# First pair of a seven-product feed-forward: evictions between weight sums, early tiles, another product order, and down weights prepared one pair later

## The chip, the cores and the metric

One core of a Trainium2 chip runs the kernel. The core has a matrix engine (PE; its weight loads are listed as PEld), a vector engine (DVE), a scalar engine (ACT), a slower general engine (POOL) and queues that start transfers between device memory and on-chip memory (here nearly all from SP). Each engine works through its own list of instructions in order and waits where an operand isn't ready. The metric is the device time of one launch in microseconds, the median of several runs.

## The reference, cut to what matters

```python
h = rms_norm(x, norm1_w) * (1.0 + scale1) + shift1
x = x + gate1 * hybrid_mixer(h, w_in, ..., w_out)      # ends in  concat[A, B] @ w_out
h = rms_norm(x, norm2_w) * (1.0 + scale2) + shift2
x = x + gate2 * swiglu(h, w_gate, w_up, w_down)
return rms_norm(x, norm_f_w)

def swiglu(h, w_gate, w_up, w_down):
    return (jax.nn.silu(h @ w_gate) * (h @ w_up)) @ w_down
```

One sequence of 1024 tokens, model width 1024, feed-forward width 2816, all in float32. The change lies where the mixer's output projection ends and the gate and up projections begin, and it touches the preparation of `w_down`.

## The kernel before

The residual stream x is held transposed after the mixer, as eight tiles of 128 features by 1024 tokens; `x2h(m, hf)` is feature tile m in token half hf (512 tokens). The page of the profile prints them as `x`.

**Products.** The gate and up projections run in 11 pairs of column tiles (256 of 2816 columns; p is the pair, q is 0 for gate and 1 for up). Each pair is a 2 by 2 block product done with seven block products instead of eight: four input blocks of the weights (A11, A12, A21, A22) and their sums S1 = A21 + A22, S2 = S1 - A11, S3 = A11 - A21, S4 = A12 - S2, against four blocks of the activations (B11, B21 from token half 0; B22 from token half 1) and their differences T1, T2, T3, T4. A float32 operand is split into a rounded high half (ACT: a CAST or an ACTIVATE) and a rest (DVE: a subtraction, called its low half below); three matmuls, high by high, high by low, low by high, make one product of a 128-row block. A block product is 24 matmuls: two q, four row blocks k, three parts.

**Accumulators.** `X`, `Y`, `Z` and `V` name pairs of PSUM banks (one for each q). X takes A11·B11, is copied out (`p1`), goes on summing S2·T2, is copied again (`u2`), then S3·T3 (`z5`) and A22·T4. V takes S1·T1 in the first pair only; Y takes A12·B21, Z takes S4·B22. `keep` copies a bank out on ACT, `close` adds a bank on DVE, `silu` and `act` make silu(gate) times up; the results go to device memory (`am_scr`), also as sums.

**The first pair** (lines 2000 to 2128 of before) is written out by hand, since its activations are made while it runs. The last two of eight column tiles of the output projection (`w_out_t`, 24 matmuls each; `o` in the profile) run on PE while DVE forms the weight sums. `evict` adds a finished column tile to x in token half 1 and lets ACT square it; `add_sq` adds the square to `sq`. After the eighth, four small matmuls sum the squares of the token half over features (`row_sums`, tile `ss`), `row_root` takes the inverse root, and a matmul spreads it (`row_bc`, tile `RS`). Then `scale` normalises a tile, and `t_make` makes B22 and the T blocks with their halves. Low halves are queued in `low_q` and issued by `lows(n)`, which leaves n pending. `run0` issues a block product in a given order of (q, k); `hooks` puts work after the given matmul.

**Later pairs** run seven steps s through `run` and `block(p, s)`; the code of step s + 1's operands is issued behind step s. In each pair from 1 on, `prep_load`, `prep_gate` and `prep_sums` prepare two row blocks of `w_down` (4 loads, 4 multiplications by the gate, 4 subtractions, 7 stores to `bm_scr`), for pair p - 1. The eleventh preparation lies in the down projection.

**The down projection** runs 21 steps n (three chunks of 4, 4 and 3 pairs, seven products each), each of four slots of 12 or 9 matmuls (`dn`); operands come back from `am_scr` and `bm_scr`, three steps ahead, and are split one step later. A product's add into `xo` on DVE comes one slot after it. `flush` issues the pending stores.

All the order around the change is that of the code; nothing reorders it.

## Time and profile before

| | |
|---|---|
| median of 3 runs | 1168.71 us (1168.21 to 1169.12) |
| the profiled execution, its own time | 1169.62 us |
| its span, first to last instruction | 1167.8 us |
| PE busy in the span | 1147.9 us (98%) |
| DVE busy | 955.1 us (82%) |
| ACT busy | 565.6 us (48%) |
| mean granted TensorE clock | 0.994 |

Rows of the timeline give the start of a run of like instructions, how long it lasts, the engine, the operation, the tile written and the tiles read, their number, and in brackets how long the engine was idle before and what released it. Windows give the busy time of each engine in a stretch, the granted clock (PEclk, 1.00 is full), and the share of the transfer engines in use.

### The profile page before, as it was taken

What the parts mean: (1) busy time and instruction counts of PE and PEld (TensorE: products, weight loads), DVE (VectorE), ACT (ScalarE), POOL (GpSimd) and SP (SyncE); (2) the same over time, 40 slices, a digit from 0 to 9 for tenths busy, and PEclk for the clock granted to TensorE, in tenths of its full rate; (3) what the DMA queues carried; (4) which work ended last, traced back from release to release, by engine and by line L of the source; (5) the groups of instructions that cost most, each with busy time, mean ns of one, the idle gap of its engine ahead of it and who ended that gap; (6) DMA issues with size and microseconds to landing.
All of it is one profiled execution on the core that took longest, in us unless ns stands there. A gap on an engine that the chain in (4) does not pass through costs nothing.

```text
span 1167.8 us, 16828 instructions
## 1 busy us (share of the span) xinstructions
PE 1147.9 (98%) x5606; PEld 961.3 (82%) x5606; DVE 955.1 (82%) x1882; ACT 565.6 (48%) x1238; POOL 55.9 (5%) x85
## 2 busy tenths in 40 slices
PE   8999999999999999989899999999999999999997
PEld 7878888988888988866788888888888888888886
DVE  6799887898998875777998788887888797788676
ACT  6689732658734642244444433443344465443343
POOL 2010101001100001000000000000000000000002
PEclk9999999999999999999999999999999999999999
DMA  9823456443455570620455666556655599969413
GB/s 370 329 74 126 152 175 202 142 147 121 128 162 164 172 253 28 118 99 1 154 188 171 195 221 214 177 160 207 230 190 158 181 316 385 330 206 340 144 36 144
DMA packets 162056, 213.38 MB, mean 183 GB/s; under 512 B 54449, under 2 KB 79025, under 8 KB 161969
## 3 DMA queue, kind: packets, MB, share of 16 engines
q1 hardware_dynamic: 159568, 211.72, 55.1%
q8 instruction: 44, 0.72, 0.3%
q10 hardware_dynamic: 2400, 0.59, 0.2%
q14 instruction: 44, 0.35, 0.1%
HBM read 154.58 MB, written 57.67 MB: 182 GB/s over the span
## 4 chain that ended last, share of the span: by engine, by line
PE 92%; DVE 4%; ACT 2%; issue 1%; DMA 0%; POOL 0%; SPq 0%; ACTq 0%
PE acc L87 33%; PE acc L448 25%; PE dn L87 17%; PE o L87 4%; PE o L448 4%; PE A L448 1%; PE K L448 1%; DVE x L88 1%; DVE xo L88 1%; PE w L448 1%; PE u L448 1%; PE qk L448 1%; PE kk L448 1%; PE O L448 1%; DMA x<-in_x_dram 0%
## 5 line engine op out<-in xcount | busy, mean ns | idle before, releaser
L448 PE MATMUL acc<-h,u 128*128 128x512 f32 x1200 | 296.9, 397 | 0.3 <-ACT pr L448 0.3
L448 PEld LDWEIGHTS acc<-h,u 128*128 128x128 f32 x1200 | 220.2, 188 | 43.4 <-ACT pr L448 0.8
L87 PE MATMUL acc<-h,hl 128*128 128x512 f32 x552 | 132.3, 395 | 0.2 <-DVE h L88 0.2
L87 PE MATMUL acc<-T,hl 128*128 128x512 f32 x528 | 127.5, 394 | 3.2 <-ACT cc L88 2.2
L87 PEld LDWEIGHTS acc<-h,hl 128*128 128x128 f32 x552 | 104.2, 190 | 23.0 <-issue 1.0
L87 PEld LDWEIGHTS acc<-T,hl 128*128 128x128 f32 x528 | 98.9, 190 | 24.3 <-ACT cc L88 2.6
L87 PE MATMUL acc<-h,u 128*128 128x512 f32 (+1 forms) x504 | 97.5, 344 | 0.0
L87 PEld LDWEIGHTS acc<-h,u 128*128 128x128 f32 x504 | 82.9, 189 | 12.6
L88 DVE TENSOR_TENSOR xo<-xo,dn 128x512 f32<-128x512 f32 x84 | 57.2, 686 | 41.8 <-PE dn L87 32.9
L87 PE MATMUL dn<-h,h 128*128 128x512 f32 x396 | 90.7, 389 | 0.0
L87 PEld LDWEIGHTS dn<-h,h 128*128 128x128 f32 x396 | 74.3, 188 | 15.4
L448 ACT CAST u<-raw 128x512 fp32r<-128x512 f32 x69 | 42.8, 620 | 63.6 <-PE acc L448 57.4
L88 DVE TENSOR_TENSOR cc<-cc,acc 128x512 f32<-128x512 f32 x68 | 42.6, 648 | 30.1 <-PE acc L87 30.1
L87 PE MATMUL acc<-T,u 128*128 128x512 f32 x264 | 63.3, 392 | 2.2 <-ACT T L88 1.3
L448 DVE TENSOR_TENSOR u<-raw,u 128x512 fp32r<-128x512 f32 x82 | 56.2, 687 | 11.1 <-ACT u L448 11.1
L87 PEld LDWEIGHTS acc<-T,u 128*128 128x128 f32 x264 | 49.3, 188 | 14.5 <-ACT T L88 2.7
L448 DVE SCALAR_TENSOR_TENSOR cv<-pr,cols_a,cv 128x512 f32<-128x512 f32 x72 | 53.3, 747 | 0.5 <-ACT cv L448 0.4
L88 ACT ACTIVATE cc<-cc 128x512 f32<-128x512 f32 x33 | 20.8, 633 | 67.6 <-DVE cc L88 67.6
L88 ACT CAST hl<-S 128x512 fp32r<-128x512 f32 x42 | 24.1, 622 | 60.3 <-DVE S L88 54.9
L88 ACT CAST u<-R 128x512 fp32r<-128x512 f32 (+1 forms) x62 | 35.3, 587 | 35.2 <-DVE R L88 35.0
L88 ACT CAST h<-rw 128x512 fp32r<-128x512 f32 x57 | 32.7, 617 | 40.5 <-PE dn L87 34.6
L88 DVE TENSOR_TENSOR hl<-S,hl 128x512 fp32r<-128x512 f32 x42 | 27.3, 689 | 26.5 <-ACT hl L88 26.5
(355 smaller groups left out, 2115.4 us busy)
## 6 DMA issues: line engine op xcount, KB each, us to landing
raw<-in_w_in_dram SPq DMA_DIRECT2D x82, 256.0 KB, 3.1
am_scr<-cc SPq DMA_DIRECT2D x77, 256.0 KB, 5.2
raw<-in_w_mod_dram SPq DMA_DIRECT2D x64, 256.0 KB, 3.2
rw<-am_scr SPq DMA_DIRECT2D x55, 256.0 KB, 5.3
rw<-bm_scr SPq DMA_DIRECT2D x53, 256.0 KB, 5.3
bm_scr<-raw SPq DMA_DIRECT2D x51, 256.0 KB, 5.5
R<-in_w_gate_dram SPq DMA_DIRECT2D x22, 512.0 KB, 4.2
R<-in_w_up_dram SPq DMA_DIRECT2D x22, 512.0 KB, 5.4
```

The lines of the kernel that those rows point to most:

```text
L87: return call(*a, **k)
L88: ins = call(*a, **k)
L448: ins = call(*a, **k)
```

## The change

In the first pair the last two evictions move up between the weight sums: the seventh right after S2, the eighth after S4's halves. The differences S3 are formed later, after the squares. Empty tiles (`room`) are named first in the new pool, which settles which addresses the later tiles get; S1's, S3's and S2's halves get tiles of their own (`cast_in`). The root and its spreading no longer sit between the matmuls of A11·B11 but behind it. After S4·B22 the product S1·T1 runs before S2·T2, so all T1 blocks are made before the T2 blocks. The order of (q, k) inside a product is 00, 01, 10, 11, 02, 03, 12, 13. X is copied to `z5` during T4, into two `raw` tiles. The closing of the first pair's Y and Z (`rest0`) moves from before pair 1 into step 1 of pair 1. The preparation of `w_down` is shifted by one pair: none in pair 1, and two instead of one in the down projection (loads at n = 7 and 9, multiplications and sums at 8 and 10, stores at 9 and 11).

```diff
     elif s == 1:  (in block)
                 if p < 2:
                     keep(p, "p1", "X")
+                if p == 1:
+                    rest0()
                 w.cast("S1", 0)
...
-            prep_gate(p - 1)
+            if p > 1:
+                prep_gate(p - 2)
...
-            prep_sums(p - 1)
+            if p > 1:
+                prep_sums(p - 2)
...
+    for tag, shape, bufs in [("S", [P, 2, 4, P], 2)] * 2 + [(f"T2_{k}", [P, 2, HT], 1) for k in range(4)] + [("L", [P, 2, HT], 1)] + \
+            [(f"{n}_{k}", [P, 2, HT], 1) for n in ("T3", "T4") for k in range(4)]:
+        mp.tile(shape, F32R if tag[0] == "T" else F32, name=nm("room"), tag=tag, bufs=bufs)
...
-    for n in ("S1", "S2", "S4", "S3"):
-        W[0].sum_n(n)
-        if n in ("S2", "S4"):
-            cast0(n, 0)
-            cast0(n, 1)
-    lows()
-    evict(M_ORD[6], ps_o[6])
...
-    ACT.activation(warm, ones[:, 0:1], AF.Sqrt)
-    add_sq()
-    evict(M_ORD[7], ps_o[7])
-    add_sq()
-    run0("A11", "B11", b0["X"], True, hooks={12: lambda: row_sums(1, 7), 20: lambda: (row_root(1), row_bc(1, 6))})
+    W[0].sum_n("S1")
+    W[0].sum_n("S2")
+    cast_in("S2", 0, "T4_0")
+    cast_in("S2", 1, "T4_1")
+    evict(M_ORD[6], ps_o[6])
+    W[0].sum_n("S4")
+    cast_in("S4", 0, "T4_2")
+    cast_in("S4", 1, "T4_3")
+    ACT.activation(warm, ones[:, 0:1], AF.Sqrt)
+    lows(2)
+    add_sq()
+    lows(1)
+    evict(M_ORD[7], ps_o[7])
+    lows()
+    add_sq()
...
+    turns = [(0, 0), (0, 1), (1, 0), (1, 1), (0, 2), (0, 3), (1, 2), (1, 3)]
+    cast_in("S1", 1, "T3_3")
+    lows()
+    W[0].sum_n("S3")
+    W[0].cast("S1", 0)
+    run0("A11", "B11", b0["X"], True, hooks={12: lambda: row_sums(1, 7)})
+    row_root(1)
+    row_bc(1, 6)
+    cast_in("S3", 0, "S", 2)
...
+    for n, make in enumerate((t1, t2, t3, t4)):
+        for k in range(4):
+            make(k)
+            lows(1)
+            if k == 0 and n == 1:
+                run0("S1", "T1", b0["V"], True, turns)
+            elif k == 0 and n == 2:
+                run0("S2", "T2", b0["X"], False, turns)
+            elif k == 1 and n == 2:
+                keep(0, "u2", "X")
+            elif k == 0 and n == 3:
+                run0("S3", "T3", b0["X"], False, turns)
+            elif k == 1 and n == 3:
+                c[0]["z5"] = [raw_t(), raw_t()]
+                for q in (0, 1):
+                    ACT.copy(c[0]["z5"][q], b0["X"][q])
...
+    def rest0():
+        close(0, "p1", "Y")
+        silu(0, "p1")
+        close(0, "u2", "Z")
+        silu(0, "u2")
+        act(0, "p1")
+        dma(am_scr[0, A_IX["A11"]], c[0]["p1"][0])
+        act(0, "u2")
...
-                prep_load(p - 1)
+                if p > 1:
+                    prep_load(p - 2)
...
+        if n in (7, 9) and i == 0:
+            prep_load(NP - 2 + (n == 9), ring)
...
+        if n in (8, 10) and i == 0:
+            prep_gate(NP - 2 + (n == 10))
+        if n in (8, 10) and i == 2:
+            prep_sums(NP - 2 + (n == 10), ring)
+        if n in (9, 11) and i == 0:
             flush()
```

On DVE, before, this stood between the weight sums S2 and the root of the norm. `R` are loaded weights (the rows that write R form S4 and S3 in place), `u` low halves of S2 and S4, `sq` the sum of squares, `x<-o` an eviction:

```order
L88 TENSOR_TENSOR R_5341<-R_5341,S_5348 128x4x128
L88 TENSOR_TENSOR R_5342<-R_5342,S_5348 128x4x128
L88 TENSOR_TENSOR R_5337<-R_5337 128x4x128
L88 TENSOR_TENSOR R_5338<-R_5338 128x4x128
L88 TENSOR_TENSOR u_5351<-S_5348,u_5351 128x512
L88 TENSOR_TENSOR u_5353<-S_5348,u_5353 128x512
L88 TENSOR_TENSOR u_5357<-R_5341,u_5357 128x512
L88 TENSOR_TENSOR u_5359<-R_5342,u_5359 128x512
L88 TENSOR_TENSOR sq_5047<-sq_5047,raw_5329 128x512
L88 SCALAR_TENSOR_TENSOR x_2_4570<-o_5277,mod_c,x_2_4570 128x512
L88 TENSOR_TENSOR sq_5047<-sq_5047,raw_5369 128x512
L88 SCALAR_TENSOR_TENSOR x_3_4571<-o_5302,mod_c,x_3_4571 128x512
```

And now, at the same place:

```order
L88 TENSOR_TENSOR sq_5047<-sq_5047,raw_5329 128x512
L88 SCALAR_TENSOR_TENSOR x_2_4570<-o_5277,mod_c,x_2_4570 128x512
L88 TENSOR_TENSOR R_5341<-R_5341,S_5360 128x4x128
L88 TENSOR_TENSOR R_5342<-R_5342,S_5360 128x4x128
L88 TENSOR_TENSOR u_5366<-S_5360,u_5366 128x512
L88 TENSOR_TENSOR u_5368<-S_5360,u_5368 128x512
L88 TENSOR_TENSOR sq_5047<-sq_5047,raw_5372 128x512
L88 TENSOR_TENSOR u_5376<-R_5341,u_5376 128x512
L88 SCALAR_TENSOR_TENSOR x_3_4571<-o_5302,mod_c,x_3_4571 128x512
L88 TENSOR_TENSOR u_5378<-R_5342,u_5378 128x512
L88 TENSOR_TENSOR sq_5047<-sq_5047,raw_5386 128x512
L88 TENSOR_TENSOR u_5406<-S_5361,u_5406 128x512
```

The seventh eviction moved ahead of six instructions, the eighth ahead of one of them and of the two that form S3, which now come later.

On ACT, before, in the same stretch (`u<-S` and `u<-R` are the high halves of S2 and S4, `raw<-x` squares an evicted tile; the brackets list the engines whose signals an instruction waits for):

```order
L88 CAST u_5351<-S_5348 128x512 [waits DVE_49,PE_49,Activation_49]
L88 CAST u_5353<-S_5348 128x512 [waits DVE_49,PE_49]
L88 CAST u_5357<-R_5341 128x512 [waits DMAHW0_49,DVE_49,PE_49]
L88 CAST u_5359<-R_5342 128x512 [waits DMAHW1_49,DVE_49]
L88 ACTIVATE raw_5369<-x_2_4570 128x512 [waits DMAHW4_49,DMAHW3_49,DMAHW5_49,DMAHW2_49,DVE_49]
L88 ACT_TABLE_LOAD
```

And now:

```order
L88 CAST u_5366<-S_5360 128x512 [waits DVE_49,Activation_49]
L88 CAST u_5368<-S_5360 128x512 [waits DVE_49,Activation_49]
L88 ACTIVATE raw_5372<-x_2_4570 128x512 [waits DMAHW4_49,DMAHW3_49,DMAHW5_49,DMAHW2_49,DVE_49]
L88 CAST u_5376<-R_5341 128x512 [waits DMAHW0_49,DVE_49]
L88 CAST u_5378<-R_5342 128x512 [waits DMAHW1_49,DVE_49,Pool_49]
L88 ACT_TABLE_LOAD
```

The square moved ahead of two casts, and the first three casts lost their wait for PE.

On DVE, before, this stood where token half 1 is normalised further (`x<-x,mod_c,RS` is `scale`; `x<-x` is the difference T1, `raw<-x,x` the difference T2, `T<-raw` the low half of T2):

```order
L88 TENSOR_TENSOR x_0_4568<-x_0_4568 128x512
L88 TENSOR_TENSOR raw_5499<-x_4_4572,x_0_4568 128x512
L88 SCALAR_TENSOR_TENSOR x_1_4569<-x_1_4569,mod_c,RS_5419 128x512
L88 SCALAR_TENSOR_TENSOR T_978_5501<-raw_5499,mod_c,T_978_5501 128x512
L88 TENSOR_TENSOR x_1_4569<-x_1_4569 128x512
L88 TENSOR_TENSOR raw_5510<-x_5_4573,x_1_4569 128x512
```

And now (`h<-x` is the low half of T1):

```order
L88 TENSOR_TENSOR x_0_4568<-x_0_4568 128x512
L88 SCALAR_TENSOR_TENSOR x_1_4569<-x_1_4569,mod_c,RS_5447 128x512
L88 TENSOR_TENSOR x_1_4569<-x_1_4569 128x512
L88 SCALAR_TENSOR_TENSOR x_2_4570<-x_2_4570,mod_c,RS_5447 128x512
L88 TENSOR_TENSOR h_1_997_5525<-x_0_4568,h_1_997_5525 128x512
L88 TENSOR_TENSOR x_2_4570<-x_2_4570 128x512
```

The T2 differences and their low halves left this place; the T1 low halves, which stood behind them, moved up to it.

More of the change, by code (lines that the diff above doesn't have):

```diff
@@ L2013, in run0, with w_low, cast_in @@
                     hooks[n_mm]()
-    def cast0(n, q):
-        if n in ("S2", "S4"):
-            u = mp.tile([P, 2, 4, P], F32R, name=nm("u"), tag="T4_" + str(q + (2 if n == "S4" else 0)), bufs=1)
-            n_slot[0] += 1
-            ACT.copy(u[:, 0], W[0].m[n][q])
-            W[0].u.setdefault(n, [None, None])[q] = u
-        else:
-            W[0].cast(n, q)
-        low_q.append(lambda: W[0].low(n, q))
-    for n in ("S1", "S2", "S4", "S3"):
-        W[0].sum_n(n)
-        if n in ("S2", "S4"):
-            cast0(n, 0)
-            cast0(n, 1)
+    def w_low(n, q):
+        low_q.append(lambda: W[0].low(n, q))
+    def cast_in(n, q, tag, bufs=1):
+        u = mp.tile([P, 2, 4, P], F32R, name=nm("u"), tag=tag, bufs=bufs)
+        n_slot[0] += 1
+        ACT.copy(u[:, 0], W[0].m[n][q])
+        W[0].u.setdefault(n, [None, None])[q] = u
+        w_low(n, q)
+    W[0].new("S2")
+    W[0].new("S1")
+    W[0].sum_n("S1")
[11 more added lines that the diff above has]
+    evict(M_ORD[7], ps_o[7])
     lows()
-    evict(M_ORD[6], ps_o[6])
+    add_sq()
     for d in spill:
@@ L2034 @@
     spill.clear()
-    ACT.activation(warm, ones[:, 0:1], AF.Sqrt)
-    add_sq()
-    evict(M_ORD[7], ps_o[7])
-    add_sq()
-    dma(*spill.pop())
-    b0 = {n: [bank_tile(2 * j + q, "acc") for q in (0, 1)] for j, n in enumerate("XY")}
-    run0("A11", "B11", b0["X"], True, hooks={12: lambda: row_sums(1, 7), 20: lambda: (row_root(1), row_bc(1, 6))})
+    b0 = {n: [bank_tile(2 * j + q, "acc") for q in (0, 1)] for j, n in enumerate("XYZ")}
+    b0["V"] = [bank_tile(6 + q, "acc") for q in (0, 1)]
+    bk[0] = [{n: b0[n][q] for n in "XYZ"} for q in (0, 1)]
+    turns = [(0, 0), (0, 1), (1, 0), (1, 1), (0, 2), (0, 3), (1, 2), (1, 3)]
[7 more added lines that the diff above has]
+    cast_in("S3", 0, "S", 2)
+    W[0].low("S1", 0)
+    lows()
     run0("A12", "B21", b0["Y"], True)
-    for q in (0, 1):
-        cast0("S1", q)
     lows()
@@ L2048 @@
         t_make("B22", k, x2h(4 + k, 1), b2c[:, 4 + k:5 + k])
-        if k < 3:
-            scale(5 + k, 1)
-        lows(1)
-    turns = [(q, k) for k in range(4) for q in (0, 1)]
-    b0["Z"] = [bank_tile(4 + q, "acc") for q in (0, 1)]
-    bk[0] = [{n: b0[n][q] for n in "XYZ"} for q in (0, 1)]
-    for k in range(4):
-        scale(k, 1)
+        scale(5 + k if k < 3 else 0, 1)
         lows()
-        if k == 0:
-            run0("S4", "B22", b0["Z"], True, turns)
+    run0("S4", "B22", b0["Z"], True, turns)
@@ L2060, with t1, t2 @@
+    keep(0, "p1", "X")
+    ACT.activation(warm, ones[:, 0:1], AF.Silu)
+    def t1(k):
         g0, g1 = x2h(k, 0), x2h(k, 1)
         DVE.tensor_tensor(g0, g1, g0, ALU.subtract)
+        if k < 3:
+            scale(k + 1, 1)
+        t_make("T1", k, g0)
+    def t2(k):
         tm[k] = raw_t()
-        DVE.tensor_tensor(tm[k], x2h(4 + k, 1), g0, ALU.subtract)
+        DVE.tensor_tensor(tm[k], x2h(4 + k, 1), x2h(k, 0), ALU.subtract)
         t_make("T2", k, tm[k], b2c[:, 4 + k:5 + k])
-        if k == 0:
-            keep(0, "p1", "X")
@@ L2067, with t3 @@
-    ACT.activation(warm, ones[:, 0:1], AF.Silu)
-    for k in range(4):
-        t_make("T1", k, x2h(k, 0))
-        lows(1)
-        if k == 0:
-            run0("S2", "T2", b0["X"], False, turns)
-    b0["V"] = [bank_tile(6 + q, "acc") for q in (0, 1)]
-    keep(0, "u2", "X")
-    for k in range(4):
+    def t3(k):
         g1 = x2h(k, 1)
         DVE.scalar_tensor_tensor(g1, x2h(4 + k, 1), db2[:, k:k + 1], g1, ALU.add, ALU.subtract)
-        if k == 0:
-            lows()
-            run0("S1", "T1", b0["V"], True, turns)
@@ L2081, with t4 @@
         t_make("T3", k, g1)
-        if k in (0, 1):
-            cast0("S3", k)
-        lows(1)
-    for k in range(4):
+    def t4(k):
         DVE.tensor_tensor(tm[k], x2h(4 + k, 0), tm[k], ALU.subtract)
-        if k == 0:
-            lows()
-            run0("S3", "T3", b0["X"], False)
         t_make("T4", k, tm[k])
-        if k in (0, 1):
-            cast0("A22", k)
-        lows(1)
+    for n, make in enumerate((t1, t2, t3, t4)):
[14 more added lines that the diff above has]
+                    ACT.copy(c[0]["z5"][q], b0["X"][q])
+            if n == 1 and k == 2:
+                cast_in("S3", 1, "S", 2)
+            if n == 3 and k == 0:
+                for q in (0, 1):
+                    W[0].cast("A22", q)
+                    w_low("A22", q)
@@ L2101 @@
     W[1].load(1)
-    keep(0, "z5", "X")
-    run0("A22", "T4", b0["X"], False, [(0, 0), (0, 1), (1, 0), (1, 1), (0, 2), (1, 2), (0, 3), (1, 3)])
+    run0("A22", "T4", b0["X"], False, turns)
     for q in (0, 1):
@@ L2107 @@
         c2, c5 = c[0]["u2"][q], c[0]["z5"][q]
+        DVE.tensor_tensor(c2, c2, b0["V"][q], ALU.add)
         DVE.tensor_tensor(c5, c5, b0["V"][q], ALU.add)
-        DVE.tensor_tensor(c2, c2, b0["V"][q], ALU.add)
-    close(0, "p1", "Y")
-    silu(0, "p1")
     silu(0, "z5")
@@ L2115 @@
     n_slot[0] += 2
-    act(0, "p1")
-    dma(am_scr[0, A_IX["A11"]], c[0]["p1"][0])
     W[1].low("A12", 0)
     W[1].low("A12", 1)
-    close(0, "u2", "Z")
-    silu(0, "u2")
     act(0, "z5")
     store(0, "A22", c[0]["z5"][0])
-    act(0, "u2")
-    a11, a21, a22, s1, s3 = c[0]["p1"][0], c[0]["u2"][0], c[0]["z5"][0], c[0]["p1"][1], c[0]["u2"][1]
-    DVE.tensor_tensor(s1, a21, a22, ALU.add)
-    DVE.tensor_tensor(s3, a11, a21, ALU.subtract)
-    store(0, "S1", s1)
-    store(0, "S3", s3)
+    def rest0():
[6 more added lines that the diff above has]
+        act(0, "u2")
+        a11, a21, a22, s1, s3 = c[0]["p1"][0], c[0]["u2"][0], c[0]["z5"][0], c[0]["p1"][1], c[0]["u2"][1]
+        DVE.tensor_tensor(s1, a21, a22, ALU.add)
+        DVE.tensor_tensor(s3, a11, a21, ALU.subtract)
+        store(0, "S1", s1)
+        store(0, "S3", s3)
     for p in range(1, NP):
@@ L2300 @@
         if n == 7 and i == 0:
-            prep_load(NP - 1, ring)
             dma(nfb, norm_f_w.partition_broadcast(P))
+        if n in (7, 9) and i == 0:
+            prep_load(NP - 2 + (n == 9), ring)
         settle(k)
         split_pair(n, i)
-        if n == 8 and i == 0:
-            prep_gate(NP - 1)
-        if n == 8 and i == 2:
-            prep_sums(NP - 1, ring)
-        if n == 9 and i == 0:
+        if n in (8, 10) and i == 0:
[3 more added lines that the diff above has]
+        if n in (9, 11) and i == 0:
             flush()
```

## The prediction, made before the changed kernel ran

> **What bounds the kernel now.** I read the windows by stage first: busy time of each engine, then the granted clock, the share of the transfer engines and GB/s.

> ```profile
> 515.00:574.00 59.00, 49.29 (x186) 36.66 (x185) 45.32 (x72) 28.19 (x48) 0.00 (x0) 0.91 0.14 45
> 574.00:1140.00 566.00, 566.00 (x2674) 476.04 (x2673) 459.22 (x737) 240.80 (x457) 0.85 (x4) 1.00 0.64 213
> ```

> From 574 to 1140 us PE (first number behind the comma) never rests and its clock is full: there nothing but fewer matmuls would help, and a later stage simply moves earlier with what precedes it. From 515 to 574, the first pair, PE rests for 10 us and its clock is 0.91. The waits of PE in that stretch and its timeline show where:

> ```profile
> PE ss L87 <- DVE sq L88: 4.1, 1, 4.1
> PE acc L87 <- ACT cc L88: 2.2, 1, 2.2
> PE acc L87 <- DVE T L88: 1.8, 5, 0.7
> ```

> ```profile
> 515.81 2.90 PE L87 MATMUL acc<-h,hl 128*128 128x512 f32 x12
> ...
> 522.80 1.39 PE L87 MATMUL ss<-ones,sq 128*128 128x1 f32 x6 [4.09 <-DVE sq L88]
> ...
> 566.35 5.97 PE L87 MATMUL acc<-T,hl 128*128 128x512 f32 x18 [2.22 <-ACT cc L88]
> ...
> 573.52 5.60 PE L87 MATMUL acc<-h,hl 128*128 128x512 f32 x24
> ...
> 584.40 5.60 PE L87 MATMUL acc<-T,hl 128*128 128x512 f32 x24
> ```

> The first pair begins at 515.81, pair 1 at 573.52 (its third product at 584.40). After 12 matmuls PE waits 4.09 us for the squares; later it waits for T blocks, and 2.22 us for the copy of X. The windows around the two long waits, and of the first two products of pair 1:

> ```profile
> 522.80:524.40 1.60, 1.60 (x8) 1.60 (x8) 0.00 (x0) 0.00 (x0) 0.00 (x0) 0.51 0.02 5
> 524.40:528.00 3.60, 3.60 (x9) 2.86 (x10) 1.47 (x3) 0.77 (x2) 0.00 (x0) 0.50 0.00 0
> ...
> 567.50:570.50 3.00, 3.00 (x8) 2.34 (x7) 3.00 (x6) 0.32 (x1) 0.00 (x0) 0.50 0.00 0
> ...
> 573.52:584.40 10.88, 10.88 (x49) 9.01 (x48) 10.04 (x15) 4.50 (x9) 0.00 (x0) 1.00 0.63 219
> ```

> Each long wait is paid twice: after it the clock is half for at least 5.2 and 3.0 us, in which 2.6 and 1.5 us of work are lost. A product of 24 matmuls at full clock takes 10.88 / 2 = 5.44 us.

> What ends the waits is a chain through DVE and ACT:

> ```profile
> 513.95 0.62 ACT L88 CAST u<-S 128x512 fp32r<-128x512 f32 x1 [7.68 <-PE o L87]
> ...
> 515.30 0.62 ACT L88 CAST u<-S 128x512 fp32r<-128x512 f32 x1 [0.73 <-PE o L87]
> ...
> 518.47 0.75 DVE L88 SCALAR_TENSOR_TENSOR x<-o,mod_c,x 128x512 f32<-128x512 f32 x1
> ...
> 519.90 1.28 ACT L88 ACT_TABLE_LOAD   x1
> ...
> 521.96 0.69 DVE L88 TENSOR_TENSOR sq<-sq,raw 128x512 f32<-128x512 f32 x1 [0.69 <-ACT raw L88]
> ...
> 541.63 0.69 DVE L88 TENSOR_TENSOR raw<-x,x 128x512 f32<-128x512 f32 x1
> ...
> 543.11 0.75 DVE L88 SCALAR_TENSOR_TENSOR T<-raw,mod_c,T 128x512 fp32r<-128x512 f32 x1
> ...
> 544.50 0.69 DVE L88 TENSOR_TENSOR raw<-x,x 128x512 f32<-128x512 f32 x1
> ```

> S2's high halves waited on PE until 513.95 and 515.30; the evictions stood behind them on DVE, and the squares ended at 522.65. Later each T2 block takes DVE 2.87 us (541.63 to 544.50), while PE needs 1.36 us for a block of S2·T2.

> **What PE needs at least.** Squares and root have their own matmuls:

> ```profile
> 475.03 0.95 PE L87 MATMUL ss<-ones,sq 128*128 128x1 f32 x8
> ...
> 480.08 1.02 PE L87 MATMUL RS<-raw,ones 128*128 128x512 f32 x2
> ```

> Seven products are 7 x 5.44 = 38.1 us; with 0.9 and 0.9 for these two (somewhat under their rows, as neighbours overlap) 39.9 us, against 573.52 - 515.81 = 57.7. So 17.8 us are lost, and the question is how much of it the new order still loses. I walk it through with these durations:

> ```profile
> 506.72 1.28 DVE L88 TENSOR_TENSOR S<-R,R 128x512 f32<-128x512 f32 x2
> ...
> 510.23 2.02 PE L87 MATMUL o<-WQ,h 128*128 128x512 f32 x8
> ...
> 515.57 0.40 PE L87 MATMUL o<-at,h 128*128 128x512 f32 x1
> ...
> 532.09 2.06 DVE L88 SCALAR_TENSOR_TENSOR x<-x,mod_c,RS 128x512 f32<-128x512 f32 x3
> ...
> 572.72 1.12 ACT L88 CAST u<-R 128x512 fp32r<-128x512 f32 x2
> ...
> 578.89 1.22 DVE L88 TENSOR_TENSOR S<-R,R 128x1024 f32<-128x1024 f32 x1
> ```

> On DVE a two-tile sum lasts 0.69 and the next starts after 0.60, one with a scalar 0.75 and 0.66; an ACT high half 0.62 and 0.52.

> **Squares.** S1 and S2 start at 506.72 as before and take DVE to 509.1; the casts no longer list PE, so ACT makes S2's halves by 509.9. The seventh column tile ends where the eighth begins, about 510.4 with the last matmul's tail; eviction done 511.2, its square on ACT 511.9. DVE goes on with S4 (2), two low halves, the add, one low half: 511.1 + 6 x 0.60 = 514.7. ACT has two casts and the table load behind it by 514.5. The eighth tile ends at 515.57 + 0.40 = 515.97; eviction done 516.75, square 517.4, add done 518.1. PE's first 12 matmuls end at 515.81 + 2.72 = 518.5. The 4.09 us wait goes, and the half clock with it; 0.4 us is left over.

> **B22 and the T blocks.** PE then: ss to 519.4, rest of A11 522.2, RS 523.1, A12 528.5, S4 533.9, S1 539.4, S2 544.8, S3 550.3, A22 555.7 if nothing waits. DVE may scale from 523.3. Nine scales and low halves of B22 take 9 x 0.66 + 0.2: 529.5, before S4 needs the last. To the second T1 block stand 5 sums and 3 scales, 5.1: 534.6; S1·T1, reading blocks 0 and 1 first, needs it at 533.9 + 0.9 = 534.8. To the last T2 block stand 8 sums and 5 scalar ones, 8.1: 542.7; needed 16 matmuls into S2·T2, at 543.0. T3's third block waits on ACT for the copy of X behind S2·T2 (545.1 + 0.5) and its own cast: low half from 546.3, last T3 block 548.2, needed 548.4. To T4's second block stand 6 more, 551.8; needed 551.2: PE waits 0.6. So pair 1 starts at 556.3. These are margins of 0.2 to 0.4, so I add 0.4 for signals between engines, which my steps leave out: 556.7.

> **Sum:** 573.52 - 556.7 = 16.8 us less. Against the profiled execution's own time, 1169.62 (span 1167.8), that is 1152.8; that execution lies 0.9 above the median of the runs, so against the median 1168.71 - 16.8 = 1151.9.

> **Edits that I cost at nothing.** `rest0` moves 8 DVE instructions (4.8 us), two silus and one store behind pair 1's first product; that pair loses the 8 of the down weights. It adds a wait: the first pair's A11 is stored and then overwritten on DVE for S2, and S1's low halves for pair 1's fourth product stand behind it on DVE. From 553.7 DVE has 17 sums and 2 wide ones to the end of that `act`, 12.6 us and some 1.6 of waits for ACT: store issued 567.9. S1's first low half ends 2.0 us after the store has landed; it is needed at 556.7 + 3 x 5.44 + 0.45 = 573.5. So up to 3.6 us of landing are free.

> ```profile
> DMA to landing us min/median/max: 2.0/5.2/8.4
> ```

> That is the view of all transfers on `am_scr`. Bounds: 0, and 8.4 - 3.6 = 4.8 us. I take 0: the queue is empty there (no share of transfers in the window 567.5 to 570.5, and pair 1's loads are then done), which is nearest to the 2.0.

> The second down-weight preparation adds 8 DVE instructions (4.8 us) and 11 transfers of 256 KB to steps 9 to 11 of the down projection:

> ```profile
> 1050.00:1060.00 10.00, 10.00 (x46) 8.29 (x45) 8.33 (x14) 3.39 (x8) 0.00 (x0) 1.00 1.02 339
> 1060.00:1070.00 10.00, 10.00 (x46) 8.29 (x45) 9.00 (x15) 4.95 (x10) 0.00 (x0) 1.00 1.05 387
> 1070.00:1080.00 10.00, 10.00 (x46) 8.29 (x45) 7.30 (x13) 2.92 (x6) 0.00 (x0) 1.00 0.87 297
> ```

> Transfers are full there: 2.9 MB at 387 GB/s are 7.4 us later landings. But operands are split at least a step (10.9 us) before use, and an add into a bank that the next step goes on filling may be late by three slots of 2.7 less its 0.7, 7.5 us; DVE's 4.8 fit. Bounds 0 and 7.4; I take 0, as PE is at 10.00 in all three rows and the lag fits each cover alone.

> **Rivals.**
> 1. *The squares stay late.* If S2's casts still ended at 514.5 and 515.9, two casts, the table load and the square behind them put the add at 520.5: PE waits 2.0. As the 2.22 us wait was followed by half clock, another 1.7 (3.4 us at half): 1155.6. Against it: those casts list no wait for PE now. [...]
> 2. *DVE becomes the bound.* It has almost no rest from 506.7 to 553.7; if 70 instructions each take 0.02 to 0.05 more, PE waits 1 to 3 us in short pieces: 1153.4 to 1155.
> 3. *The down projection pays* for the late preparation, 2 to 7.4 us: 1154 to 1159.3.
> 4. *Nothing comes of it:* the rooms only move the waits, another address conflict holds PE as long. 1168.7. Against it: PE's own list of waits names no new operand.
> 5. *Slower than before:* step 10's multiplications wait on DVE for `w_down` tiles that come late behind full queues, with four products' adds behind them, and PE stops at step 11. The price is the lag less 7.5 us; it passes the 16.8 gained plus 2.3 (0.2%) only from a lag of 26.6 us, against 4.8 for the work itself.

> **How the numbers follow.** Forecast (1150.6 to 1153.4) 0.60; rival 1 0.11, rival 2 0.14, rival 3 0.10, rival 4 0.02, rival 5 0.03. The time is the forecast's, 1151.9. Below it at most the 0.6 wait and the 0.4 allowance can vanish, and runs spread by 0.5: low 1150.4. Upward it takes in rivals 1 and 2 and half of rival 3: high 1157.0. About 0.2% (2.3 us) is what runs tell from no change: faster 0.95, within 0.02, slower 0.03.

> **What would show it.** Right: no wait of PE on `sq`, clock 1.00 through the first pair, pair 1's first product some 40.9 us after the first A11 matmul, PE without rest from there to the tail. Wrong: a wait of PE over 1 us there with half clock behind it; a DVE wait on a transfer of `am_scr` in pair 1 with PE waiting for S1; PE below 10.00 in the windows of steps 10 to 12.

## The result, and the profile after

| | before | after |
|---|---|---|
| median (4 runs each, same job) | 1168.46 us (1167.55 to 1169.12) | 1153.24 us (1152.63 to 1153.64) |
| ratio, with its 95% interval | | 0.987 (0.9853 to 0.9887) |
| the profiled execution, its span | 1169.62, 1167.8 us | 1153.19, 1151.4 us |
| PE busy in the span | 1147.9 us (98%) | 1140.3 us (99%) |
| DVE busy | 955.1 us | 953.4 us |
| first A11 matmul to pair 1's first product | 57.71 us | 40.96 us |
| from there to the end of the span | 594.28 us | 594.09 us |

The forecast was 1151.9 us in 1150.4 to 1157.0, and 40.9 us for the first pair.

First the windows by stage of the kernel after, with the columns of the prediction's windows: the first pair, pair 1, and the rest up to the tail.

```profile
515.00:556.00 41.00, 40.65 (x180) 32.56 (x179) 37.53 (x61) 22.64 (x39) 0.00 (x0) 1.00 0.18 58
556.00:574.00 18.00, 18.00 (x81) 14.92 (x80) 16.24 (x25) 6.68 (x12) 0.00 (x0) 1.00 0.28 103
574.00:1120.00 546.00, 546.00 (x2587) 459.42 (x2586) 445.04 (x717) 236.13 (x446) 0.84 (x4) 1.00 0.65 217
```

PE rests 0.35 us in 41, and the clock is 1.00 where it was 0.91. From 556 on PE never rests, as before, so the later stages only moved earlier.

PE's timeline of the kernel after (start, duration, engine, operation, tiles, and in brackets the idle time and its releaser):

```profile
516.35 2.90 PE L87 MATMUL acc<-h,hl 128*128 128x512 f32 x12
519.09 0.95 PE L87 MATMUL ss<-ones,sq 128*128 128x1 f32 x8
...
552.62 4.85 PE L87 MATMUL acc<-T,hl 128*128 128x512 f32 x20 [0.32 <-DVE T L88]
557.31 4.92 PE L87 MATMUL acc<-h,hl 128*128 128x512 f32 x21
```

The row of `ss` has no bracket: the wait of 4.09 us is gone. The one bracket left in the first pair is 0.32 us, at T4's second block. A bracket counts from the modelled end of the matmul before it, so what a wait costs is better read from start to start: A22·T4 takes 557.31 - 551.15 = 6.16 us and needs 5.44, so 0.7 is lost there.

And the chain through ACT and DVE that ended that wait, in the timeline after:

```profile
509.23 1.22 ACT L88 CAST u<-S 128x512 fp32r<-128x512 f32 x2 [2.43 <-DVE S L88]
...
510.97 0.75 DVE L88 SCALAR_TENSOR_TENSOR x<-o,mod_c,x 128x512 f32<-128x512 f32 x1 [0.62 <-PE o L87]
...
516.55 0.75 DVE L88 SCALAR_TENSOR_TENSOR x<-o,mod_c,x 128x512 f32<-128x512 f32 x1 [1.22 <-PE o L87]
...
517.33 0.63 ACT L88 ACTIVATE raw<-x 128x512 f32<-128x512 f32 x1 [2.20 <-DVE x L88]
...
518.00 0.69 DVE L88 TENSOR_TENSOR sq<-sq,raw 128x512 f32<-128x512 f32 x1
```

S2's casts now wait for DVE's sum and no longer for PE, the evictions start as soon as PE has finished a column tile, and the last add of squares ends at 518.69, 0.4 us before PE reads it.

The two spans differ by 16.4 us: 16.75 in the first pair, 0.19 behind it, less 0.54 because this execution began its first pair later (516.35 against 515.81). The stage ahead isn't touched by the change, and that start spreads: over the profiled executions of all kernels below it lies between 514.08 and 516.73.

### The profile page after: what moved, and what is told of

Read it like the earlier page. It is cut to its first block, busy times and chain, and to the rows that moved or that the text cites. A ratio compares the mean times of both kernels' runs of the same rounds, so it can differ in the third digit from the quotient of the medians.

```text
span 1151.4 us, 16808 instructions
## 1 busy us (share of the span) xinstructions
PE 1140.3 (99%) x5606; PEld 957.9 (83%) x5606; DVE 953.4 (83%) x1882; ACT 566.8 (49%) x1238; POOL 55.9 (5%) x85
## 4 chain that ended last, share of the span: by engine, by line
PE 94%; DVE 2%; ACT 1%; DMA 1%; issue 1%; POOL 0%; SPq 0%; ACTq 0%; DVEq 0%
PE acc L87 36%; PE acc L448 24%; PE dn L87 17%; PE o L87 4%; PE o L448 4%; PE A L448 1%; PE K L448 1%; DVE xo L88 1%; PE u L448 1%; PE w L448 1%; PE qk L448 1%; PE kk L448 1%; PE O L448 1%; DMA x<-in_x_dram 0%; DVE h L448 0%
## 5 line engine op out<-in xcount | busy, mean ns | idle before, releaser
L87 PE MATMUL acc<-h,hl 128*128 128x512 f32 x540 | 127.4, 391 | 0.0
L87 PE MATMUL acc<-T,hl 128*128 128x512 f32 x504 | 119.9, 390 | 0.3 <-DVE T L88 0.3
L87 PEld LDWEIGHTS acc<-h,hl 128*128 128x128 f32 x540 | 100.6, 188 | 21.4 <-issue 0.5
L87 PEld LDWEIGHTS acc<-T,hl 128*128 128x128 f32 x504 | 93.3, 188 | 19.5 <-DVE T L88 0.8
L87 PE MATMUL acc<-h,u 128*128 128x512 f32 (+1 forms) x516 | 100.5, 344 | 0.0
L87 PEld LDWEIGHTS acc<-h,u 128*128 128x128 f32 x516 | 85.0, 189 | 13.1
L87 PE MATMUL dn<-h,h 128*128 128x512 f32 x396 | 90.7, 389 | 0.0
L88 DVE TENSOR_TENSOR xo<-xo,dn 128x512 f32<-128x512 f32 x84 | 57.0, 684 | 37.6 <-PE dn L87 29.6
L87 PEld LDWEIGHTS dn<-h,h 128*128 128x128 f32 x396 | 74.3, 188 | 15.4
L448 ACT CAST u<-raw 128x512 fp32r<-128x512 f32 x69 | 42.8, 620 | 62.8 <-PE acc L448 57.0
L88 DVE TENSOR_TENSOR cc<-cc,acc 128x512 f32<-128x512 f32 x66 | 41.4, 645 | 31.4 <-PE acc L87 31.4
L87 PE MATMUL acc<-T,u 128*128 128x512 f32 x288 | 67.1, 389 | 0.0
L448 DVE TENSOR_TENSOR u<-raw,u 128x512 fp32r<-128x512 f32 x82 | 56.3, 687 | 11.0 <-ACT u L448 10.9
L87 PEld LDWEIGHTS acc<-T,u 128*128 128x128 f32 x288 | 54.1, 188 | 11.2
L88 ACT CAST h<-rw 128x512 fp32r<-128x512 f32 x60 | 34.5, 618 | 47.7 <-PE dn L87 40.2
L88 ACT CAST u<-R 128x512 fp32r<-128x512 f32 x64 | 36.5, 587 | 41.0 <-DVE R L88 38.7
L88 ACT CAST hl<-S 128x512 fp32r<-128x512 f32 x41 | 23.5, 620 | 54.6 <-DVE S L88 53.8
L88 ACT ACTIVATE cc<-cc 128x512 f32<-128x512 f32 x32 | 20.3, 633 | 59.7 <-DVE cc L88 59.7
L448 DVE SCALAR_TENSOR_TENSOR raw<-raw,cb 128x512 f32<-128x512 f32 x64 | 43.5, 681 | 3.6 <-DMA raw<-in_w_mod_dram 3.3
```

What stands on the lines that cost most here:

```text
L87: return call(*a, **k)
L88: ins = call(*a, **k)
L448: ins = call(*a, **k)
```

## The experiments

Each is an edit of the kernel after. "Region" is the time from the first A11 matmul to pair 1's first product (40.96 us after), "rest" that from there to the end of the span (594.09). The time is the median of four executions for r0, u2, u1 and f1, and that of one execution for the others; region and rest are those of the one execution profiled.

| run | edit | time, us | region | rest |
|---|---|---|---|---|
| r0_again | none | 1152.05 | 40.91 | 594.09 |
| u4_sums_first | evictions behind the sums | 1152.38 | 40.98 | 594.18 |
| u3_no_room | no `room` | 1154.36 | 42.86 | 594.19 |
| u3_again | the same | 1154.69 | 42.88 | 594.21 |
| u34_neither | both | 1160.21 | 47.61 | 594.06 |
| u5_t2_first | S2·T2 before S1·T1 | 1153.17 | 41.86 | 594.12 |
| u6_z5_late | copy `z5` behind T4 | 1156.75 | 45.21 | 594.15 |
| u2_close_back | `rest0` before pair 1 | 1154.35 | 40.97 | 595.73 |
| u1_prep_back | `w_down` not shifted | 1155.43 | 40.97 | 596.71 |
| f1_prep_two_later | `w_down` shifted by two | 1152.82 | 40.96 | 594.16 |
| d3_three_more | three more DVE instructions | 1155.37 | 44.32 | 594.2 |
| d3_again | the same | 1156.03 | 44.34 | 594.13 |

**Is the later start the program's?** The kernel after, unchanged, with four timed runs:

> The changed kernel once more, as a control. Theory: the first pair (first A11 matmul to pair 1's first matmul) takes 40.9 to 41.0 us again and the time is 1153 us; the 0.54 us by which the first pair began later than in the run of before (516.35 against 515.81) is spread between executions and comes out anywhere within 0.6. Rival: the later start belongs to the changed program and comes back as 516.3 to 516.4.

Measured: 1152.05 us (1151.91 to 1152.62), ratio 0.986 (0.9845 to 0.9875); before in the same job 1169.11. PE's timeline of this run:

```profile
515.30 2.90 PE L87 MATMUL acc<-h,hl 128*128 128x512 f32 x12
...
556.21 5.60 PE L87 MATMUL acc<-h,hl 128*128 128x512 f32 x24
```

The first pair began 1.05 us earlier than in the first profile of the same kernel, and took the same time to 0.05 us. That is more than the 0.6 expected, and the rival's 516.3 didn't come back. So where it begins differs from execution to execution. In what follows I compare region and rest, in which that spread isn't.

**The squares: evictions or addresses?** Three runs take away the one, the other, and both.

```diff
-    evict(M_ORD[6], ps_o[6])          # u4: both evictions behind S4 and its halves
     W[0].sum_n("S4")
...
+    lows()
+    evict(M_ORD[6], ps_o[6])
...
-    for tag, shape, bufs in [("S", ...)]:     # u3: no room
-        mp.tile(..., name=nm("room"), ...)
```

> Only the order of the evictions is undone (both stand behind the sums S1, S2, S4 and their low halves), the empty tiles stay. Theory: with the casts free of PE the sums and halves are done by 513.9, the eighth column tile ends at 516.5 and sets the squares as in the changed kernel: no wait of PE, 0 us. Rival: the eviction order is what removes the wait, and it comes back: 2 to 7.7 us over.

> Only the empty tiles are left out, the order is that of the changed kernel. Theory: S2's high halves wait again for PE (until about 514.5 and 515.8), the squares end about 520.9, PE waits 1.9 us (1.5 to 2.5) for them and then runs at half clock for some 3.4 us: 3.6 us over the changed kernel. [...] Rival 2: the addresses do not matter and the order of the evictions is what counts: 0.

> Neither the empty tiles nor the new order of the evictions. Theory: the squares end about 523.2, PE waits 4.2 us (3.5 to 4.8) and runs at half clock for some 7 us behind it: 7.5 us over the changed kernel, all that this place lost before. Rival: S3's later sums alone bring the squares forward by 1.2 us: a wait under 3 us, 5 us over or less.

Without `room`, the evictions still between the sums, a cast on ACT (u3_no_room, timeline) waits again just as long as in before:

```profile
513.69 0.62 ACT L88 CAST u<-S 128x512 fp32r<-128x512 f32 x1 [7.68 <-PE o L87]
...
515.04 0.62 ACT L88 CAST u<-S 128x512 fp32r<-128x512 f32 x1 [0.73 <-PE o L87]
```

and PE's timeline of the same run, then of u34_neither:

```profile
520.13 1.02 PE L87 MATMUL ss<-ones,sq 128*128 128x1 f32 x8 [1.67 <-DVE sq L88]
```

```profile
523.73 1.84 PE L87 MATMUL ss<-ones,sq 128*128 128x1 f32 x8 [4.09 <-DVE sq L88]
```

and last PE's timeline of u4_sums_first, where the row of `ss` has no bracket:

```profile
518.19 0.95 PE L87 MATMUL ss<-ones,sq 128*128 128x1 f32 x8
```

With the addresses settled, the place of the evictions is worth nothing (u4: region 40.98). With the old addresses it is worth much: 1.67 us of waiting with the evictions moved, 4.09 without, the very wait of before. S3's sums, which in u34 no longer stand ahead of the evictions, bring the squares no closer, against the rival there. In u3 the half clock that was expected didn't come, and the region grew by 1.9, the expected length of the wait alone; why is worked out below. Both u3 and u34 keep the tiles of their own (`cast_in`), so these alone don't help. It is `room`, which computes nothing, that removes the wait (with `cast_in` in place; `room` without it was not run); the moved evictions alone would have softened it.

**The order of the products.** T2 blocks and S2·T2 ahead of the T1 blocks and S1·T1; the copy `u2` moves with S2·T2, and the order of (q, k) inside a product stays new.

```diff
-    for n, make in enumerate((t1, t2, t3, t4)):
+    for n, make in enumerate((t12, t1_last, t3, t4)):
...
-                run0("S1", "T1", b0["V"], True, turns)
+                run0("S2", "T2", b0["X"], False, turns)
```

> Only the order of the products is undone: T2 blocks are made with the differences and S2·T2 runs ahead of S1·T1. Theory: a T2 block takes DVE 2.87 us against 1.36 us of PE, the last is ready about 541.6 and 1.8 us of matmuls stand behind it: S2·T2 ends at 543.4 where the changed kernel's second product ends at 540.2; 3 us (2 to 4) over, in waits under 1.5 us each, at full clock. Rival: the new order of blocks (0, 1 of both q first) and not the order of products gave the gain: under 1 us over.

PE's timeline there, S2·T2 and the first matmuls of S1·T1 behind it, and then the same two places in before:

```profile
533.62 1.07 PE L87 MATMUL acc<-T,u 128*128 128x512 f32 x4
536.12 4.99 PE L87 MATMUL acc<-T,u 128*128 128x512 f32 x20 [1.44 <-DVE T L88]
540.95 1.53 PE L87 MATMUL acc<-h,hl 128*128 128x512 f32 x6
```

```profile
541.54 2.09 PE L87 MATMUL acc<-T,u 128*128 128x512 f32 x7
...
550.92 0.47 PE L87 MATMUL acc<-h,hl 128*128 128x512 f32 x1
```

The region grew by only 0.9. From start to start S2·T2 loses 1.9 us, around its one wait of 1.44, and the 1.0 that other products lose in the kernel after vanishes (S4·B22 0.2, S1·T1 0.1, A22·T4 0.7). The expectation of 2 to 4 us was too high, and its rival, under 1 us, right in number. S2·T2 takes 7.3 us (533.62 to 540.95) where it took 9.4 in before (541.54 to 550.92) and needs 5.44. So half of that loss is got back even with the products in the old order; by which of the remaining edits (the order of (q, k), the scales and halves that DVE does between the blocks) was not taken apart.

**The copy of X.**

```diff
-            elif k == 1 and n == 3:
-                c[0]["z5"] = [raw_t(), raw_t()]
...
+    keep(0, "z5", "X")
     run0("A22", "T4", b0["X"], False, turns)
```

> Only the early copy of X to z5 is undone: it stands behind the last T4 block again. Theory: A22·T4 cannot start before about 554.4 where S3·T3 ends at 551.15: PE waits 3.2 us (2.5 to 3.5) and then has half clock for 3.4 us; less the 0.3 us wait of the changed kernel that is 4.5 us over (3.5 to 5). Rival: the copy is not the bound, T4's second block is: under 0.5 us over.

PE's timeline, and two windows set on the edges at which the clock changed (explained below):

```profile
553.66 7.36 PE L87 MATMUL acc<-T,hl 128*128 128x512 f32 x24 [3.04 <-ACT cc L88]
```

```profile
551.40:554.81 3.41, 1.15 (x5) 0.98 (x6) 2.52 (x5) 2.82 (x6) 0.00 (x0) 1.00 0.47 157
554.81:558.22 3.41, 3.41 (x10) 2.64 (x9) 3.41 (x6) 1.98 (x4) 0.00 (x0) 0.50 0.00 0
```

From start to start the wait of 3.04 us costs 3.2 us, and 3.41 us at half clock another 1.7; less the 0.7 that A22·T4 loses in the kernel after, that is 4.2, measured 4.25. The early copy is worth that much.

**Closing and `w_down`.** The closing back before pair 1; the preparation of `w_down` back in pair 1; and the preparation a further pair later, so that three lie in the down projection.

```diff
-                if p == 1:                     # u2: called before the loop over pairs
-                    rest0()
...
-            if p > 1:                          # u1: p - 1; f1: p > 2 and p - 3
-                prep_gate(p - 2)
+            prep_gate(p - 1)
```

> Only rest0 is undone: the first pair's Y and Z are closed before pair 1's first block, as before. Theory: 8 DVE instructions (4.8 us) stand ahead of the last reading of X, which frees the banks of pair 1's second product, and ahead of S2's sums: PE waits 0.5 us before the second product and 0.3 to 1 us in the third, no half clock; 1 us (0.5 to 2) over the changed kernel. Rival: nothing is lost, as DVE had room: 0.

> Only the shift of the down weights is undone: pair 1 prepares again (its loads one pair step later, since two of their tiles hold z5 until then), and one preparation is left in the down projection. Theory: the shift is worth nothing by itself, DVE has room in both places: time as the changed kernel within 1 us, PE without rest in pairs 1 to 10. Rival: pair 1 cannot carry rest0's 8 DVE instructions and the 8 of the preparation (9.6 us): PE waits 1 to 4 us in pair 1 or 2.

> The preparation is shifted by two pairs: three of eleven lie in the down projection, at its steps 5 to 11. Theory: still 0, since DVE's lag of 4.8 us for each is under the 7.5 us that an add may be late, and PE stays at full time from step 5 to 12; time as the changed kernel within 1 us. Rival: transfers are full there and each preparation that lies in the down projection costs 2 to 7 us, so this one is 2 to 7 us slower than the changed kernel.

u2_close_back, PE's timeline:

```profile
569.20 5.73 PE L87 MATMUL acc<-T,hl 128*128 128x512 f32 x24 [0.95 <-ACT cc L88]
```

Closed ahead of pair 1, the first pair's results keep ACT and DVE from pair 1's work, and PE starts its second product 0.3 us later and its third another 1.2: with that, 1.6 us more in the rest. In before the closing stood there too, and the preparation in pair 1 besides, and the rest was 594.28 us. So what the closing costs at its old place depends on what stands around it; that the wait of 2.22 us ahead of pair 1 hid it in before is likely, but was not tested. u1_prep_back, the waits of PE and then DVE's timeline:

```profile
PE acc L87 <- ACT L L88: 1.3, 1, 1.3
PE acc L87 <- DVE cc L88: 0.7, 1, 0.7
```

```profile
581.76 2.49 DVE L88 TENSOR_TENSOR raw<-raw,gate 128x512 f32<-128x512 f32 x4
...
587.22 1.41 DVE L88 TENSOR_TENSOR raw<-raw,raw 128x512 f32<-128x512 f32 x2
588.55 0.69 DVE L88 TENSOR_TENSOR bt<-raw,raw 128x512 f32<-128x512 f32 x1
589.27 0.69 DVE L88 TENSOR_TENSOR bt<-raw,bt 128x512 f32<-128x512 f32 x1
589.88 1.27 DVE L88 TENSOR_TENSOR cc<-cc,acc 128x512 f32<-128x512 f32 x2
```

Here my theory, that nothing would be lost, was wrong and the rival right: the rest grew by 2.6 us (ratio to before 0.9889, 0.9874 to 0.9904; the unchanged kernel 0.986 in the same job). Of the eight `w_down` instructions the last four stand right ahead of the adds into `cc` at 589.88; PE, which these adds release, stops for 0.7 us, and in pair 2, behind an ACT that is late in turn, for another 1.3; from start to start the two cost 1.0 and 1.6 us. (In this kernel the loads of pair 1 come at s = 2, since the early copy holds two of the tiles that they use; DVE has no wait for them.) Three preparations in the down projection cost nothing: rest 594.16, and PE is at 10.00, without a wait, in all six windows of 10 us from 1020 to 1080. One of the windows of f1_prep_two_later, with the transfers full:

```profile
1050.00:1060.00 10.00, 10.00 (x46) 8.29 (x45) 9.93 (x18) 6.37 (x11) 0.00 (x0) 1.00 1.05 396
```

**What a wait costs in clock.** u3_no_room waited 1.67 us at full clock, against 2.22 us in before with half clock behind it. To see whether length decides, three repetitions of an S4 low half put the squares late by about as much; then both kernels ran once more.

```diff
     evict(M_ORD[7], ps_o[7])
     lows()
+    for _ in range(3):
+        W[0].low("S4", 1)
     add_sq()
```

> The changed kernel with one low half of S4 worked out three times more ahead of the last add of the squares: 1.8 us more on DVE. Theory: 0.4 us of it is cover, PE waits 1.4 to 1.5 us for the squares; whether the clock falls after a wait of this length is what the run is for: 1.5 us over if not, 3.2 over if it falls for 3.4 us. [...]

> The kernel without the empty tiles once more. In its first run PE waited 1.67 us for the squares and its clock stayed at 1.00. Theory: whether a wait of this length halves the clock hangs on where it falls in a window of the clock's own that runs on whatever the program does, so each execution draws anew: full clock (first pair 42.9 us) or half (44.4) are both open. Rival: it belongs to the program, and the clock is full again.

> The kernel with three low halves more, once more. In its first run PE waited 1.57 us for the squares and ran at half clock behind it. Theory: as for the other repeat, each execution draws anew: first pair 44.3 us at half clock or 42.8 at full. Rival: it belongs to the program (the instructions around the wait), and the clock is half again.

d3 waited 1.57 us in both its runs and lost the clock both times; u3 waited 1.67 and 1.68 and kept it both times. So length alone doesn't decide, and both repeats came out as their rival said, as if the program did. The traces' record of the clock speaks against that. In each of the 14 executions profiled (before, after, and the runs above), every change of the clock up to the end of the down projection lies a whole number of steps of 3.413 us behind the first full clock. In before the full clock first came at 7.42 us, and the changes at 522.83, 529.65, 567.20 and 570.61 lie 151, 153, 164 and 165 steps behind it. So I cut the span into these slots. The windows of u3_again, then of d3_again, slot by slot:

```profile
516.34:519.75 3.41, 2.38 (x11) 1.62 (x9) 2.97 (x6) 3.38 (x7) 0.00 (x0) 1.00 0.11 42
519.75:523.17 3.42, 2.77 (x16) 2.50 (x17) 3.38 (x7) 1.58 (x4) 0.00 (x0) 1.00 0.09 35
523.17:526.58 3.41, 3.41 (x14) 2.45 (x14) 2.30 (x4) 0.61 (x1) 0.00 (x0) 1.00 0.00 0
```

```profile
518.55:521.97 3.42, 1.85 (x13) 1.67 (x13) 3.37 (x7) 1.32 (x3) 0.00 (x0) 1.00 0.00 0
521.97:525.38 3.41, 3.41 (x10) 2.63 (x9) 1.90 (x3) 0.07 (x1) 0.00 (x0) 0.50 0.00 0
525.38:528.79 3.41, 3.41 (x15) 2.46 (x14) 2.08 (x4) 1.39 (x2) 0.00 (x0) 1.00 0.00 0
```

In u3 an edge of the slots cut the wait in two, and PE was busy 0.70 and 0.81 of the slots; in d3 the whole wait fell into one, busy 0.54, and the next slot ran at 0.50. The same in their first runs (0.71 and 0.80; 0.56). So in these runs what the wait emptied of one slot decided, and with it the wait's place against the slots. That place isn't the program's: counted from the first full clock, the kernel after began its first pair at 509.23 us in one run and 507.84 in the other. u3 began it at 508.09 and 508.06, d3 at 509.04 and 509.18. Each fell twice at nearly the same place; that each agreed with itself I put down to luck. No kernel was seen with both outcomes, so that one execution keeps the clock and the next loses it is worked out, not seen. An estimate from the same traces, with the slots laid over PE's times at every place: d3 would have a slot of 0.56 or less in 58% of them, u3 in 61%.

## Why the prediction was right, and where its steps were off

**What PE needs at least, and the walk.** 39.9 us at least and 40.9 with what remains; measured 40.96 and, unchanged, 40.91. Squares with 0.4 us to spare: 0.4. One wait at T4's second block, 0.6: the bracket says 0.32, and from start to start A22·T4 loses 0.7. The other margins of 0.2 to 0.4, on which the walk depended for three products, held: PE has no other wait in the list. S4·B22 and S1·T1 take 5.63 and 5.54 us for 5.44, together 0.3, within the 0.4 allowed for signals. Rival 2, in which DVE falls a little behind with each of 70 instructions, didn't happen.

**The sum.** 16.8 predicted, 16.75 measured. The median came out at 1153.24 instead of 1151.9, and at 1152.05 in the other job: in the executions profiled the difference lies ahead of the first pair, in a start that moves by more than a microsecond, and the allowance of 0.5 for the spread was too small.

**Rival 1, squares late.** It didn't happen, since the casts no longer wait for PE. u3_no_room is what it describes: a wait of 1.67 for the 2.0 supposed. Its price for the clock, 1.7 us, is right where a slot is lost (d3: 1.57 of wait and 1.7 make 3.3, measured 3.36 in the region) and wrong where none is (u3: 1.9 in all). "As the 2.22 us wait was followed by half clock" was one case taken for a rule. The clock granted behind the wait was 0.50 after 1.57 us in d3 and after 2.22 in before, and 1.00 after 1.67 in u3.

**Edits costed at nothing.** For `rest0` the store's landing was to stay within its 3.6 us. The waits of DVE after:

```profile
DVE cc L88 <- DMA am_scr<-cc: 0.2, 1, 0.2
```

DVE's overwriting instruction waited 0.2 us, and PE didn't wait. Nor did the late preparation cost anything (rest 594.09 for 594.28), and f1 shows that a third one would not either, so rivals 3 and 5 were far away. The lag of 7.4 us allowed for as an upper bound wasn't seen by PE in any run.

**What the prediction left out.** It says of the shift only that "that pair loses the 8 of the down weights", and prices what the shift may cost. It never asks what its absence costs: u1 shows 2.6 us. The closing's move into pair 1 (worth 1.6 us, by u2) and the shift belong together: with the closing and the preparation both in pair 1, as in u1, those 2.6 are lost. Whether the closing's move alone would still beat moving neither is not shown, as no run with the faster first pair has both at their old places.

**Which part did it.** Against the kernel after, taken away alone: old addresses and old place of the evictions together 6.65, the early copy 4.25, the product order 0.9; together 11.8 of 16.75. PE's timelines of before and after, from each product's start to the next, show where the rest lies:

| us | before | after |
|---|---|---|
| A11·B11, squares, root and A12·B21 | 20.29 | 12.75 |
| S4·B22 | 5.44 | 5.63 |
| S2·T2 | 9.38 | 5.44 |
| S1·T1 | 6.05 | 5.54 |
| S3·T3 and the wait behind it | 9.38 | 5.44 |
| A22·T4 | 7.17 | 6.15 |

The 6.65 stand against 7.5 in the first row, the 4.25 against 5.0 in the last two. The 0.9 is what is left of 1.8 lost in S2·T2 and S1·T1, where the gain is 4.5. So some 5 us, more than half of them in S2·T2 and S1·T1, belong to what was not taken away alone. No version tried beats the kernel after beyond the spread of its start; about 1 us over PE's need is left in the first pair.

## What to carry to other kernels

Where a cast of one operand waits on an engine that has nothing to do with it, ask what lived at its addresses: reserving the addresses was worth more than the reordering beside it (region 42.86 us without the addresses, 40.98 without the reordering, 40.96 with both). Before work is moved into a stage, count what that engine already does there, and price the move and what makes room for it as one. And judge a wait of the matrix engine by where it falls, not by its length alone: in these runs 1.57 us inside one slot of 3.413 us was followed by half clock, and 1.67 us that an edge cut in two was not. As an estimate from the 3.413 us and from the busy shares of 0.56 and 0.58 below, a wait would need some 1.5 us within one slot to cost the clock; above some 3 us it would have them wherever it falls, and in between it may cost double in one execution and single in the next.

## What the runs showed of the hardware

```profile
532.81:536.22 3.41, 1.98 (x10) 1.32 (x8) 3.41 (x7) 1.45 (x2) 0.00 (x0) 1.00 0.00 0
536.22:539.64 3.42, 3.42 (x15) 2.63 (x16) 3.25 (x6) 2.21 (x5) 0.00 (x0) 1.00 0.00 0
```

These shares are taken from busy times whose ends are modelled, so 0.56 and 0.58 are rough, and no slot lies between them. The windows of before on its own slots show both its losses:

```profile
516.00:519.41 3.41, 2.71 (x12) 1.88 (x10) 3.20 (x5) 1.30 (x3) 0.00 (x0) 1.00 0.00 0
519.41:522.83 3.42, 0.03 (x1) 0.06 (x1) 2.05 (x3) 2.49 (x4) 0.00 (x0) 1.00 0.41 152
522.83:526.24 3.41, 3.41 (x12) 3.11 (x13) 1.26 (x3) 0.77 (x2) 0.00 (x0) 0.50 0.00 1
526.24:529.65 3.41, 3.41 (x8) 1.99 (x6) 0.21 (x1) 0.00 (x0) 0.00 (x0) 0.50 0.00 0
...
563.79:567.20 3.41, 1.19 (x6) 0.72 (x5) 2.67 (x5) 2.62 (x6) 0.00 (x0) 1.00 0.48 161
567.20:570.61 3.41, 3.41 (x10) 2.67 (x9) 3.27 (x6) 0.62 (x2) 0.00 (x0) 0.50 0.00 0
```

After the second wait one slot is at half clock, as in d3 and u6. After the first, with a slot all but empty, two are, though PE was busy through the whole first of them. Two are at half clock in u34_neither as well, but there the wait ran on into the first of them (PE busy 1.65 of 3.41 us). Why two in before stays open; no other execution has an empty slot.
